# One kernel, one change: spreading the roots of the front's norms by a transpose, four masked copies and one product

## The chip, the cores and the metric

The kernel runs on one core of one Trainium2 chip. A core has five engines with instruction queues of their own: TensorE (PE in the profile; its weight loads are listed apart as PEld), VectorE (DVE), ScalarE (ACT), GpSimd (POOL) and SyncE (SP), which here only issues DMAs. The engines meet through semaphores. SBUF holds 128 partitions; PSUM has eight banks of 128 x 512 float32 into which TensorE writes.

The metric is the device time of one execution in microseconds. The kernel before was timed three times; its median is 1887.86 us.

## The reference, cut to what matters

One decoder block over 2048 tokens of width 1024. Every norm divides a token's row by the root of its mean square.

```python
def rmsnorm(x, g):
    r = lax.rsqrt(jnp.mean(xf * xf, axis=-1, keepdims=True) + EPS)
    return (xf * r * g).astype(x.dtype)

hn = rmsnorm(h, norm1_g)
proj = hn @ w_in                      # u_pool | q | k | v
y_pool = pool_mixer(u_pool, pool_w, pool_scale)
o = stick_breaking_attention(q, k, v)
mixed = concat([rmsnorm(y_pool, pool_out_g), rmsnorm(y_attn, attn_out_g)])
h = h + mixed @ w_out
hn2 = rmsnorm(h, norm2_g)
h = h + square(relu(hn2 @ w_up)) @ w_down
return rmsnorm(h, final_g)
```

## The kernel before, in words

All arithmetic is float32. The tokens stand along the free dimension, in four blocks of `T` = 512 (`NT` = 4); features lie on the 128 partitions. Each float32 operand of a product is split into a rounded part and the rest (`split`: a copy by ScalarE at L147, a subtraction by VectorE at L148), and a product is three matmuls on those parts (`products`, L179 to L181 in the front).

The program falls into the front, the up projection (L1135) and the down projection (L1308, L1485). The **front** holds the input projection, the pooling mixer, the attention (`near_unit`, L642 to L709) and the output projection with its residual. Its granules of work are listed in `prog` and emitted one after the other by `run`; between two of them, `catch_up` takes small pieces out of a list `later`, and `advance` takes pieces of attention. The Tile framework then orders each engine's instructions at build time, in a list schedule that runs on estimated durations; what stands in `tc.high_priority()` goes ahead of other work that is ready. On the chip each engine runs its instructions in that fixed order and waits where a semaphore makes it.

**A norm's root** takes these steps. Squares are summed over the features' chunks into a tile of 128 x 512 (`add_square`). `mean_squares` (L207) multiplies four 128 x 128 blocks of that sum by a column of 1/n: in PSUM there is then, for each of the four token blocks of 128, one column with one token to a partition. `inv_root` computes the inverse root in 128 x 4 elements, on GpSimd for all norms but the first (L223 to L226). The result is split into `yr`, 128 x 2 x 4: rounded part and rest, for each of four token blocks.

To be used, the root has to stand along the free dimension, on every partition. `to_all` does this: it takes a PSUM tile `pr`, calls `spread` (L233), and ScalarE copies `pr` to a tile `r` (L258). In `spread`, for each block and part, one column of `yr` is broadcast to 128 columns as the weights and multiplied with the identity: eight matmuls of 128 x 128, the two parts of a block adding up in its 128 columns of `pr`. VectorE then multiplies a chunk by its gain and by `r` (`normed`, L278; `put`, L862).

`to_all` is called fourteen times: for the first norm of block 0 directly from `inv_rms`, with VectorE as the engine of the root and the tag `px`; and thirteen times through `later_rms`, with a PSUM tile of the pools `pst` or `psz`: the first norm of blocks 1 to 3, the pooling norm and the attention norm of four blocks each, the second norm of blocks 0 and 1. The pools `pst` and `psz` have two banks each and are shared with the attention's transposes (L690) and logits (L642). After the spread, a gate makes the dense products that come twelve ticks later in `prog` stand behind it in TensorE's order.

The second norm of blocks 2 and 3 (L1143) and the last norm (L1360) call `spread` from the up and down projections. They are not part of `to_all`.

The pools of the front are opened in `open_pools`; `wp` is the last of its pools in SBUF on the right side. The constants stand in `const`; `ident` and `identr` are a 128 x 128 identity, and `gap` is an unused tile that keeps the places of what follows.

Of the kernel before, what the change touches and what calls it, by code (L numbers as in the profile page):

```python
# [8 lines left out]
F32 = mybir.dt.float32  # L9
F32R = mybir.dt.float32r  # L10
BF16 = mybir.dt.bfloat16
I32 = mybir.dt.int32
AF = mybir.ActivationFunctionType
ALU = mybir.AluOpType

P = 128
S = 2048
D = 1024
T = 512
# [8 lines left out]
TB = T // P  # L28
# [17 lines left out]
def hymba_block(ctx: ExitStack, tc: tile.TileContext, xT, gains, w_in, pool_w, w_out, w_up, w_down, out):  # L46
    nc = tc.nc
# [3 lines left out]
    const = pool("const", 1)  # L51
    vp = pool("vp", 2)
    dram = pool("dram", 1, space=bass.MemoryType.DRAM)
    wp = hpb = hpa = pa = bigp = x0p = ntp = tmp = att = psd = psx = psz = pst = pso = olp = accp = acc2p = acc3p = None

    def open_pools(scope):
        nonlocal hpb, wp, tmp, ntp, psd, psx, psz, pst, pso
        fpool = lambda name, bufs, **kw: scope.enter_context(tc.tile_pool(name=name, bufs=bufs, **kw))
        hpb = fpool("hpb", KD, side="right")
        ntp = fpool("ntp", 3, side="right")  # L60
        tmp = fpool("tmp", 2, side="right")
        wp = fpool("wp", 2, side="right")
        psz = fpool("psz", 2, space=PS)
        pso = fpool("pso", 1, space=PS)
        psd = fpool("psd", 2, space=PS)
        psx = fpool("psx", 1, space=PS)
        pst = fpool("pst", 2, space=PS)
# [19 lines left out]

    front_scope, left_scope, att_scope, out_scope, last_scope, inner = (ctx.enter_context(ExitStack()) for _ in range(6))
    open_pools(front_scope)
    open_big(left_scope)  # L90

# [3 lines left out]
    ident = const.tile([P, P], F32, name="ident")  # L95
    make_identity(nc, ident)
    identr = const.tile([P, P], F32R, name="identr")
    nc.vector.tensor_copy(identr, ident)
    const.tile([P, P // 2], F32, name="gap")
    later_keys = const.tile([P, 2, 2, P], mybir.dt.int8, name="later_keys")  # L100
    nc.gpsimd.memset(later_keys, 0.0)
    for i in range(2):
# [51 lines left out]
    marks, gates = {}, []  # L154
# [47 lines left out]
    def mean_squares(parts, n, where=None, tag="px"):  # L202

        pm = (where or psx).tile([P, T], F32, tag=tag, name="pm")
        for c in range(TB):
            for i, ss in enumerate(parts):
                marks["pm"] = nc.tensor.matmul(pm[:, c:c + 1], ss[:, c * P:(c + 1) * P], inv[n],  # L207
                                               start=(i == 0), stop=(i == len(parts) - 1))
        return pm[:, 0:TB]

    def inv_root(pm, eng):

        v, w = vp.tile([P, 3 * TB], F32, tag="v", name="v"), pm.shape[-1]
        m, y, t = v[:, 0:w], v[:, TB:TB + w], v[:, 2 * TB:2 * TB + w]
        nc.vector.tensor_scalar(m, pm, 1.0, EPS, op0=ALU.mult, op1=ALU.add)
        eng.tensor_scalar(y.bitcast(I32), m.bitcast(I32), -0.5, float(0x5F3759DF), op0=ALU.mult, op1=ALU.add)
        for _ in range(3):
            if eng is nc.vector:
                eng.scalar_tensor_tensor(t, y, -0.5, y, op0=ALU.mult, op1=ALU.mult)
                eng.tensor_tensor(t, t, m, ALU.mult)  # L220
                eng.scalar_tensor_tensor(y, t, 1.5, y, op0=ALU.add, op1=ALU.mult)
            else:
                eng.tensor_tensor(t, y, y, ALU.mult)  # L223
                eng.tensor_tensor(t, t, m, ALU.mult)
                eng.tensor_scalar(t, t, -0.5, 1.5, op0=ALU.mult, op1=ALU.add)
                eng.tensor_tensor(y, y, t, ALU.mult)  # L226
        return y

    def spread(pr, yr):

        for b in range(TB):
            for x in range(2):
                mm = nc.tensor.matmul(pr[:, b * P:(b + 1) * P], yr[:, x, b:b + 1].to_broadcast([P, P]), identr,  # L233
                                      start=(b == 0 and x == 0), stop=(b == TB - 1 and x == 1), skip_group_check=True)
        return mm

    def inv_rms(ss, n, r=None, eng=None, early=False):

        eng = eng or nc.gpsimd
        with tc.high_priority():  # L240
            y = inv_root(mean_squares([ss], n, psz if early else None, "pz" if early else "px"), eng)
            yr = tmp.tile([P, 2, TB], F32R, tag="yr", name="yr")
            eng.tensor_copy(yr[:, 0], y)
            eng.tensor_tensor(yr[:, 1], y, yr[:, 0].bitcast(F32), ALU.subtract)
            if eng is nc.vector:
                return to_all(yr, r, psx, "px")
            gates.append((state["tick"] + 10, marks["pm"]))
            return yr

    def to_all(yr, r, where, tag):  # L250
        with tc.high_priority():
            pr = where.tile([P, T], F32, tag=tag, name="pr")
            marks["pr"] = spread(pr, yr)
            if tag != "px":
                gates.append((state["tick"] + 12, marks["pr"]))
            if r is None:
                r = tmp.tile([P, T], F32, tag="r", name="r", bufs=2)
            nc.scalar.activation(r, pr, AF.Copy)  # L258
            return r

    def later_rms(at, key, ss, n, r=lambda: None, early=False):

        got = {}
        where = (psz, "pz") if early else (pst, "pt")
        later.append(lambda: got.update(yr=inv_rms(ss(), n, early=early)))
        later.append(None)
        later.append(lambda: at.update({key: to_all(got["yr"], r(), *where)}))

    def rms(chunks):
        return inv_rms(sum_squares(chunks), len(chunks) * P)  # L270
# [42 lines left out]
    todo, begun, finished, state = [], {}, set(), {"gran": 0, "tick": 0, "due": 0.0}  # L313
# [37 lines left out]
    def norm1_first():  # L351

        x, h = st[0]["x"], []
        for k in range(KD):
            d = make_h(0)
            a = nc.scalar.activation(d[:, 0], x[:, k], AF.Copy, scale=g1[:, k:k + 1])
            v = nc.vector.scalar_tensor_tensor(d[:, 1], x[:, k], g1[:, k:k + 1], d[:, 0].bitcast(F32),
                                               op0=ALU.mult, op1=ALU.subtract)
            h.append((d[:, 0], d[:, 1]))
        st[0]["h"] = h  # L360
        with tc.issue_after(a.ins), tc.issue_after(v.ins):
            ss = sum_squares([x[:, k] for k in range(KD)])
        st[0]["r"] = inv_rms(ss, D, root_tile(), nc.vector)
# [1247 lines left out]
    pa = inner.enter_context(tc.tile_pool(name="pa", bufs=2))  # L1611
    x0p = x0_scope.enter_context(tc.tile_pool(name="x0p", bufs=2, side="right"))
# [10 lines left out]
    with tc.If(got < count):  # L1623
        wlist.clear(), raws.clear(), grans.clear(), gates.clear(), marks.clear()
        state["gran"], last_split[0], last_mm[0], done[:] = 0, None, None, (None, None)
        open_pools(front_scope)
        open_big(left_scope)
        open_att(att_scope)
        for j in range(NT):
            far(j)  # L1630
        att_scope.close()
        open_last(front_scope, last_scope)
        open_out(out_scope)
        tail(False)
        run()
        ffn()
# [45 lines left out]
```

## Time and profile before

| | us |
|---|---|
| median of three runs | 1887.86 |
| the three runs | 1887.64 to 1891.71 |
| the profiled execution | 1888.39 |
| its span | 1886.4 |
| mean granted clock of TensorE | 0.997 |

The profile is that of one execution. Its span runs from the first to the last instruction; the time of an execution holds about 2 us more. A matmul's duration overlaps with its neighbours', so what it costs TensorE is read from the distance between starts on the timeline. In the rows of the views, a line such as L179 is a line of the kernel; then come the engine, the operation, the tiles written and read, the shape and the count. Behind a bar stand the busy time and the mean duration in ns, behind another bar the idle time of the engine before it and what ended it. In the rows of waits stand the waiter, what it waited for, the sum, the count and the longest, in us. On the timeline stand the start, the duration, and in brackets the engine's idle time before with what ended it.

### The profile page before, as it was taken

The numbers are of one execution on the slowest core, as the hardware profiler recorded it, in microseconds if no ns is written. First come the engines' busy times: TensorE is split into PE (matmuls) and PEld (weight loads), VectorE is DVE, ScalarE is ACT, GpSimd is POOL, SyncE is SP. The second block draws the span as 40 slices with busy tenths as digits, with TensorE's granted clock in tenths as the row PEclk, the third lists the DMA queues.
The fourth block names the chain that finished last, engine by engine and source line by source line (L and its number), as shares of the span: only waits on it lengthen the run. The fifth ranks groups of instructions, "written<-read, shape, count | busy, mean of one in ns | idle before, by whom it ended". The sixth has DMA issues, their size and how long they took to land.

```text
span 1886.4 us, 26655 instructions
## 1 busy us (share of the span) xinstructions
PE 1862.2 (99%) x8883; PEld 1550.0 (82%) x8883; DVE 1470.3 (78%) x2135; ACT 1024.9 (54%) x1616; POOL 227.8 (12%) x463
## 2 busy tenths in 40 slices
PE   9999999999999999999999999999999999999997
PEld 7888888888888888778888888887888888888886
DVE  6897889678866976777899988886666677888774
ACT  6565676466543554545566555554333665656543
POOL 0232234213311140000000000000010010020120
PEclk9999999999999999999999999999999999999998
DMA  6686796799796867888898988889999898999852
GB/s 225 221 269 186 236 294 206 254 338 304 273 370 226 319 202 272 312 282 286 309 357 299 341 293 284 290 298 335 372 325 333 269 320 306 331 304 344 283 202 92
DMA packets 222164, 535.91 MB, mean 284 GB/s; under 512 B 26048, under 2 KB 32192, under 8 KB 218176
## 3 DMA queue, kind: packets, MB, share of 16 engines
q1 hardware_dynamic: 217264, 525.46, 80.0%
q0 software_dynamic: 4608, 8.39, 2.5%
q8 instruction: 72, 1.18, 0.3%
q14 instruction: 76, 0.62, 0.1%
q10 hardware_dynamic: 144, 0.26, 0.0%
HBM read 349.46 MB, written 184.55 MB: 283 GB/s over the span
## 4 chain that ended last, share of the span: by engine, by line
PE 48%; DMA 6%; DVE 3%; issue 1%; ACT 1%; POOL 0%; SPq 0%; DVEq 0%; ACTq 0%
PE pb L1308 14%; PE pY L1135 12%; PE pb L1485 12%; PE pZ L1135 6%; PE pX L1135 3%; DMA ar<-sd 1%; DMA ar<-sdi 1%; DMA hn<-hs 1%; PE pb L1425 1%; DMA b<-in_w_down_dram 1%; DVE hw L148 0%; DMA td<-t 0%; DMA sdi<-a 0%; DMA t<-in_w_down_dram 0%; DMA rb<-in_w_up_dram 0%
## 5 line engine op out<-in xcount | busy, mean ns | idle before, releaser
L1135 PE MATMUL pY<-sa,hw 128*128 128x512 f32 x1536 | 366.5, 390 | 2.5 <-ACT u L1058 2.5
L1135 PEld LDWEIGHTS pY<-sa,hw 128*128 128x128 f32 x1536 | 287.8, 188 | 64.3 <-ACT u L1058 4.4
L1308 PE MATMUL pb<-ad,wd 128*128 128x512 f32 x1344 | 305.2, 389 | 0.4 <-DVE ad L148 0.4
L179 PE MATMUL pd<-h,hl 128*128 128x512 f32 x752 | 295.9, 394 | 1.2 <-DVE qk L148 1.1
L1308 PEld LDWEIGHTS pb<-ad,wd 128*128 128x128 f32 x1344 | 252.1, 188 | 53.4 <-DVE ad L148 1.1
L180 PE MATMUL pd<-h,hl 128*128 128x512 f32 x752 | 295.7, 393 | 0.0
L181 PE MATMUL pd<-h,hl 128*128 128x512 f32 x752 | 295.2, 393 | 0.0
L1485 PE MATMUL pb<-ad,wd 128*128 128x512 f32 x1104 | 253.9, 390 | 0.8 <-ACT ad L147 0.8
L1485 PEld LDWEIGHTS pb<-ad,wd 128*128 128x128 f32 x1104 | 206.5, 188 | 44.6 <-ACT ad L147 1.2
L148 DVE TENSOR_TENSOR ad<-ar,ad 128x1024 fp32r<-128x1024 f32 x160 | 194.0, 1220 | 42.8 <-ACT ad L147 42.4
L147 ACT ACTIVATE ad<-ar 128x1024 fp32r<-128x1024 f32 x160 | 168.9, 1057 | 92.6 <-PE pb L1485 31.9
L1135 PE MATMUL pZ<-sa,hw 128*128 128x512 f32 x768 | 186.9, 390 | 1.8 <-DVE a L1078 1.8
L1135 PEld LDWEIGHTS pZ<-sa,hw 128*128 128x128 f32 x768 | 143.8, 188 | 33.2 <-DVE a L1078 3.4
L147 ACT ACTIVATE hl<-raw 128x512 fp32r<-128x512 f32 x168 | 104.4, 629 | 116.7 <-PE pd L181 75.9
L179 PEld LDWEIGHTS pd<-h,hl 128*128 128x128 f32 x752 | 141.4, 188 | 28.5 <-DVE qk L148 1.5
L181 PEld LDWEIGHTS pd<-h,hl 128*128 128x128 f32 x752 | 141.3, 188 | 28.1
L180 PEld LDWEIGHTS pd<-h,hl 128*128 128x128 f32 x752 | 141.4, 188 | 25.9
L148 DVE TENSOR_TENSOR hl<-raw,hl 128x512 fp32r<-128x512 f32 x168 | 114.9, 689 | 50.5 <-ACT hl L147 49.2
L1052 ACT ACTIVATE a<-a 128x512 f32<-128x512 f32 x96 | 60.1, 629 | 95.2 <-DVE a L1094 42.2
L148 DVE TENSOR_TENSOR hw<-rt,hw 128x512 fp32r<-128x512 f32 x128 | 86.4, 684 | 24.4 <-ACT hw L147 24.3
L147 ACT ACTIVATE wd<-wq 128x1024 fp32r<-128x1024 f32 x56 | 59.5, 1063 | 77.4 <-PE pb L1308 67.0
L148 DVE TENSOR_TENSOR wd<-wq,wd 128x1024 fp32r<-128x1024 f32 x56 | 68.4, 1222 | 35.6 <-ACT wd L147 34.1
(224 smaller groups left out, 2709.7 us busy)
## 6 DMA issues: line engine op xcount, KB each, us to landing
ar<-sd SPq DMA_DIRECT2D x96, 512.0 KB, 5.7
ar<-sdi SPq DMA_DIRECT2D x64, 512.0 KB, 5.6
rb<-in_w_up_dram SPq DMA_DIRECT2D x30, 1024.0 KB, 6.6
sd<-a SPq DMA_DIRECT2D x104, 256.0 KB, 5.3
raw<-in_w_in_dram SPq DMA_DIRECT2D x50, 512.0 KB, 4.8
sdi<-hr SPq DMA_DIRECT2D x96, 256.0 KB, 5.4
wr<-in_w_down_dram SPq DMA_DIRECT2D x48, 512.0 KB, 5.6
sd<-s SPq DMA_DIRECT2D x88, 256.0 KB, 4.8
```

What stands on the lines that cost most here:

```text
L147: nc.scalar.activation(hi, src, AF.Copy)
L148: return nc.vector.tensor_tensor(lo, src, hi.bitcast(F32), ALU.subtract)
L179: nc.tensor.matmul(ps, hl[:, 0, c], hi, start=(k == 0), stop=False)
L180: nc.tensor.matmul(ps, hl[:, 0, c], lo, start=False, stop=False)
L181: last_mm[0] = nc.tensor.matmul(ps, hl[:, 1, c], hi, start=False, stop=(k == n - 1))
L1052: nc.scalar.activation(t, src, AF.Relu)
L1135: nc.tensor.matmul(t, w[:, wx, c], a[:, ax, c % 2], start=first and c == 0 and x == 0, stop=last and c == G - 1 and x == 2, skip_group_che ...
L1308: nc.tensor.matmul(b, t[:, wx, 2 * (kk % 2) + c, i * P:(i + 1) * P], a[:, ax, c], start=p in ("P1", "P5", "P2") and kk == 0 and c == 0 and ...
L1425: nc.tensor.matmul(b[:, cols], block(t, wx, c, n), a[:, ax, c, cols], start=False, stop=(i == 1 and c == 1 and x == 2), skip_group_check=True)
L1485: nc.tensor.matmul(ps[q, n], block(t, wx, c, n), left_[q][:, ax, c], start=(n_ in ("P1", "P3") and kk == 0 and c == 0 and x == 0), stop=(n ...
```

## The change

Thirteen of the fourteen calls of `to_all` (all but the one with the tag `px`) go through a new function, `spread_rows`. It transposes `yr`, seen as 128 x 8 columns (part by block), into eight rows of 128 in the first 128 columns of `pr`. ScalarE then copies these rows four times, into the four column blocks of a tile `roots` of 128 x 512, each time with a scale from a column of `sel` that is one for the two rows of that block and zero for the others. `roots` is zero elsewhere, so one product with weights of ones, over all 128 rows, adds the two parts of each token's root and puts the sum on every partition. It writes the whole of `pr`. ScalarE copies `pr` to `r` as before.

`roots` is one tile, cleared by GpSimd when the pools are opened. `sel` and the column of ones are two small constants, made by VectorE at the start; `gap` shrinks by their size.

```diff
+        roots = fpool("zp", 1, side="right").tile([P, T], F32R, name="roots")
+        nc.gpsimd.memset(roots.bitcast(F32), 0.0)
...
-    const.tile([P, P // 2], F32, name="gap")
+    const.tile([P, P // 2 - 8], F32, name="gap")
+    sel = const.tile([P, TB], F32, name="sel")
+    nc.vector.tensor_tensor(sel, ident[:, 0:TB], ident[:, TB:2 * TB], ALU.add)
+    oner = const.tile([P, TB], F32R, name="oner")
+    nc.vector.tensor_scalar(oner, sel, 0.0, 1.0, op0=ALU.mult, op1=ALU.add)
...
+    def spread_rows(pr, yr, r):
+
+        rows = 2 * TB
+        nc.tensor.transpose(pr[0:rows, 0:P], yr.bitcast(F32).rearrange("p x b -> p (x b)"), ident)
+        for b in range(TB):
+            nc.scalar.activation(roots[0:rows, b * P:(b + 1) * P], pr[0:rows, 0:P], AF.Copy, scale=sel[0:rows, b:b + 1])
+        mm = nc.tensor.matmul(pr, oner[:, 0:1].to_broadcast([P, P]), roots, start=True, stop=True)
+        nc.scalar.activation(r, pr, AF.Copy)
+        return mm
...
     def to_all(yr, r, where, tag):
         with tc.high_priority():
             pr = where.tile([P, T], F32, tag=tag, name="pr")
-            marks["pr"] = spread(pr, yr)
-            if tag != "px":
-                gates.append((state["tick"] + 12, marks["pr"]))
             if r is None:
                 r = tmp.tile([P, T], F32, tag="r", name="r", bufs=2)
-            nc.scalar.activation(r, pr, AF.Copy)
+            if tag == "px":
+                marks["pr"] = spread(pr, yr)
+                nc.scalar.activation(r, pr, AF.Copy)
+            else:
+                marks["pr"] = spread_rows(pr, yr, r)
+                gates.append((state["tick"] + 12, marks["pr"]))
             return r
```

More of the change, by code (lines that the diff above doesn't have):

```diff
@@ L53, in hymba_block @@
     dram = pool("dram", 1, space=bass.MemoryType.DRAM)
-    wp = hpb = hpa = pa = bigp = x0p = ntp = tmp = att = psd = psx = psz = pst = pso = olp = accp = acc2p = acc3p = None
+    wp = hpb = hpa = pa = bigp = x0p = ntp = tmp = att = psd = psx = psz = pst = pso = olp = accp = acc2p = acc3p = roots = None
     def open_pools(scope):
-        nonlocal hpb, wp, tmp, ntp, psd, psx, psz, pst, pso
+        nonlocal hpb, wp, roots, tmp, ntp, psd, psx, psz, pst, pso
         fpool = lambda name, bufs, **kw: scope.enter_context(tc.tile_pool(name=name, bufs=bufs, **kw))
```

## The prediction

> **What bounds the kernel now.** I read the page's first part, then the busy time of the two halves of the span, the waits of PE in the first of them, the answer for the line of the spreading product, and the timeline around single spreads. First the page: the span, then busy time, share and count of each engine.
>
> ```profile
> span 1886.4 us, 26655 instructions
> ...
> PE 1862.2 (99%) x8883; PEld 1550.0 (82%) x8883; DVE 1470.3 (78%) x2135; ACT 1024.9 (54%) x1616; POOL 227.8 (12%) x463
> ```
>
> The view of windows, split where the front ends (columns PE, PEld, DVE, ACT, POOL busy, then clock, DMA share, GB/s):
>
> ```profile
> 0.00:610.00 610.00, 604.05 (x3247) 509.68 (x3248) 482.38 (x776) 352.18 (x635) 153.42 (x356) 1.00 0.79 262
> ```
>
> TensorE runs without a break: 604.05 of the first 610 us, at the full clock. ScalarE has 610 − 352 = 258 us free there, VectorE 610 − 482 = 128 us. The waits of PE in the same 610 us, all of them:
>
> ```profile
> PE pzero L346 <- DVE zero L94: 1.5, 1, 1.5
> PE pd L494 <- ACT h L356: 1.1, 2, 0.6
> PE pd L179 <- DVE qk L148: 1.1, 2, 0.8
> PE po L702 <- DVE ot L660: 0.7, 1, 0.7
> PE pd L495 <- DVE h L357: 0.6, 2, 0.3
> PE pta L690 <- DVE at L148: 0.5, 1, 0.5
> PE pta L690 <- DVE sg L684: 0.4, 1, 0.4
> ```
>
> That is 5.9 us in ten waits, of which 3.2 us (L346, L494, L495) are the start. So in the front a microsecond less of work for PE is a microsecond less of time, as long as the order of its instructions leaves no new hole. Who waits in a spread (the answer for L233):
>
> ```profile
> L233 PE MATMUL pr<-identr,yr x136: 220/274/326, 36.2 to 1843.6; 128*128 128x128 f32 x136
> ...
> its engine sat idle before it (us, times) until:
>   POOL yr L1353: 2.2, 2
> who waited for it (us, times):
>   ACT r L258: 12.8, 9
>   ACT rf L1360: 4.0, 2
>   ACT ra L258: 1.8, 1
> ```
>
> 136 products are 17 spreads of 8: three of the last stage (L1360), which stay, and 14 through `to_all`. One of these has the tag `px` (the first block, 36 us) and keeps `spread`. **Thirteen change**, all before 607 us. PE waited for no front root (the two waits for `yr` are L1353's, at the end); ScalarE, in turn, stood waiting for the spread in ten cases, 14.6 us in all.
>
> **The change, part by part.** PE first. One spread of before on the timeline:
>
> ```profile
> 179.09 0.39 PE L180 MATMUL pd<-h,hl 128*128 128x512 f32 x1
> ...
> 179.31 0.39 PE L181 MATMUL pd<-h,hl 128*128 128x512 f32 x1
> ...
> 179.54 1.00 PE L233 MATMUL pr<-identr,yr 128*128 128x128 f32 x8
> ...
> 180.38 0.63 PE L690 MATMUL pta<-ident,sg 128*128 128x128 f32 x4
> ...
> 180.76 0.48 PE L179 MATMUL pd<-h,hl 128*128 128x512 f32 x1
> ```
>
> Durations overlap, so the cost on PE is the distance between starts. The eight small products hold PE from 179.54 to 180.38: **0.84 us**. A 128x512 product takes 179.31 to 179.54 = **0.23 us**. Four transposes against `ident`, of the kind that is added, take 180.38 to 180.76: 0.38/4 = **0.10 us** each. The new form is one such transpose and one 128x512 product: 0.10 + 0.23 = 0.33 us. Saved per spread 0.84 − 0.33 = 0.51 us; **13 × 0.51 = 6.6 us**.
>
> Bounds: the added transpose has only 8 columns of weights, which no row shows. The nearest narrower one has 64:
>
> ```profile
> 113.66 1.01 PE L233 MATMUL pr<-identr,yr 128*128 128x128 f32 x8
> ...
> 114.51 0.34 PE L702 MATMUL po<-at,vw 128*64 128x128 f32 x2
> ...
> 114.68 0.39 PE L181 MATMUL pd<-h,hl 128*128 128x512 f32 x1
> ...
> 114.70 0.60 ACT L258 ACTIVATE r<-pr 128x512 f32<-128x512 f32 x1 [2.94 <-PE pr L233]
> ```
>
> 0.17/2 = 0.085 us. (The same rows show a handoff: the spread ends at 114.67 and ScalarE, which had stood for 2.94 us, starts at 114.70.) At most the transpose costs its whole duration of 0.27 us (the 274 ns of L233's row) and the product its 0.39 us, with nothing overlapped: saving 0.84 − 0.66 = 0.18, 2.3 us in all. At least the transpose costs nothing: 0.61, 7.9 us. I take 0.10, the row of the same operation.
>
> The Trainium skill ("TensorE: Matmul & The Clock Gate", section "LDWEIGHTS (loading the stationary operand)") has the load of weights take its columns over 1.2 GHz, so 7 ns for 8 columns, and a 128-column stream about 56 ns. By these two figures the transpose would cost 0.06 us and the sum be 7.2 us; the trace's 64-column pair, at 0.085 us, costs more than its stream alone, so I stay with the row.
>
> ScalarE gets four more instructions per spread. Rows of the groups of ScalarE's instructions in the first 620 us (busy, mean ns | idle before):
>
> ```profile
> L147 ACT ACTIVATE at<-pta 128x512 fp32r<-128x512 f32 x56 | 33.3, 597 | 9.1 <-PE pta L690 7.7 <-PE po L702 1.0
> ...
> L425 ACT ACTIVATE yb<-pp,gains 128x512 f32<-128x512 f32 x16 | 11.0, 686 | 7.0 <-PE pp L424 6.9
> ...
> L258 ACT ACTIVATE r<-pr 128x512 f32<-128x512 f32 x12 | 7.2, 596 | 12.8 <-PE pr L233 12.8
> ...
> L463 ACT ACTIVATE vf<-pd 128x512 f32<-128x512 f32 x12 | 7.2, 596 | 17.3 <-PE pd L181 17.3
> ...
> L147 ACT ACTIVATE at<-pta 128x384 fp32r<-128x384 f32 x8 | 3.9, 493 | 1.7 <-PE pta L690 1.6
> ```
>
> From 512 to 384 columns 597 − 493 = 104 ns go, so 128 columns take 597 − 3 × 104 = 285 ns; a scale from a tile adds 686 − 596 = 90 ns (L425 against L258): an estimate of 0.375 us, four of them 1.5 us. Bounds: 1.1 us if the scale costs nothing at this size, 2.4 us if columns don't matter. 13 × 1.5 = 20 us more on ScalarE lie in its 258 free us. The closing copy (L258) stays.
>
> The path from `yr` to `r` grows: transpose 0.27, masks 1.5, two handoffs of 0.03, product 0.39, against 1.0 us for the eight: about 1.2 us later, plus what the product queues behind other work on PE. Who takes `r` are VectorE's multiplications (L278, L862); they come in program order, and none of PE's waits above is for what they make (`h`, `mix`), so I cost the later `r` at nothing and keep it as rival 2.
>
> At the start POOL clears a tile and VectorE makes two small constants. The timeline of the start:
>
> ```profile
> 0.94 0.53 POOL L101 MEMSET later_keys<- 128x512 int8 x1
> ...
> 5.45 0.69 DVE L148 TENSOR_TENSOR hl<-raw,hl 128x512 fp32r<-128x512 f32 x1 [3.20 <-ACT hl L147]
> ```
>
> A memset of 512 columns is 0.53 us; VectorE stands 3.2 us idle before 5.45, waiting for ScalarE and its load. I cost this at nothing; without that cover it would be about 0.7 us. The new 2 KB tile moves later tiles of the front by a multiple of 256 bytes, the smaller `gap` keeps the constants behind it in place: nothing.
>
> Sum: the profiled execution took 1888.39 us (span 1886.4 and 2.0 around it); 1888.39 − 6.6 = 1881.8, and I say **1882.0**, 0.3% under the median of 1887.86, which stands 0.5 us below the profiled execution.
>
> **The rivals.** (1) *The product makes PE wait.* PE takes its instructions in order; between transpose and product the order of the program, fixed at build time from estimated durations, must hold enough other matmuls. On the chip the masks need 0.27 + 1.5 + two handoffs, together 1.85 us, 8 products of 0.23 us. With k products between, PE stands 1.85 − 0.23k us per spread, and from k = 5 down (0.70 us) that is more than the 0.51 saved. With k = 0 it is 13 × (1.85 − 0.51) = +17.4 us: 1906; with k = 3 it is 13 × (1.16 − 0.51) = +8.5: 1897; with k = 5 or 6 it is 1888. Beside it stands the Trainium skill (same page, "Step-by-step: what each phase is for"): only weight loads are pulled ahead, matmuls stay in program order, so that all work behind the product would stand too.
> Against it speaks the nearest chain of PE, one ScalarE instruction and PE that the trace has, a copy `vf` and its transposes, at the shortest of its 12 times:
>
> ```profile
> 356.40 0.59 ACT L463 ACTIVATE vf<-pd 128x512 f32<-128x512 f32 x1
> ```
>
> ```profile
> 359.49 0.38 PE L466 MATMUL ptv<-ident,vf 128*128 128x128 f32 x2
> ```
>
> The copy ended at 356.99, its taker started 2.5 us later, so the planned order leaves more room than the chip needs: over 3 us for one instruction of 0.6. None of the ten waits above is for such a copy (L466), nor for a root. For it speaks that a root is put ahead of all other work as soon as it counts as ready, and that four short instructions may be estimated closer than one long one. If ScalarE comes late to the masks, PE waits too: in four of fourteen spreads it was not waiting for PE.
>
> (2) *The later `r` costs elsewhere.* VectorE and ScalarE wait in order for the roots; the rows above show 14.6 us of such waits on ScalarE. A second wait, for the product behind the masks, may double them, and holds the PSUM bank, shared with the transposes of attention, some 2 us longer. If a third of 13 × 1.5 = 20 us came through to PE, it would be 6.5 us: 1888, no change.
>
> (3) *The sum is right, but the planned order falls differently.* The ten waits above were worth 2.7 us after the start; other ones of that size move the time by 2 us to either side.
>
> (4) *The change doesn't do what it says*, if the work saved were not on the path. With 604 of 610 us busy I give this nothing.
>
> **How the numbers follow.** Forecast, 1880 to 1884: 0.58. Rivals 1 and 2 at break-even, 1884 to 1891.6: 0.27. Rival 1 with few products between, 1892 to 1906: 0.13. A larger gain, by the bound of 7.9 us and luck in the order, under 1880: 0.02. A measurement of this kernel can tell about 0.2%, 3.8 us: faster than 1884.1 is 0.60, within 0.27, slower than 1891.6 0.13. The range of 8 in 10 leaves out the slower case and the far low end, and runs from **1879.5 to 1890**.
>
> **What would show it.** Right: 13 transposes and 13 products of 128x512 in place of 104 small ones, none of them in the waits of PE; PE's busy time in the front some 6.6 us shorter and the first product of the next stage that much earlier. The masks at 0.3 to 0.4 us each. Wrong: a wait of PE for the masked tile (rival 1), or new waits of PE for split tiles or PSUM banks, with VectorE or ScalarE standing for `pr` or `r` (rival 2); or a transpose or product that costs more than 0.33 us together.

## The result, and the profile after

The change made the kernel slower. Over eight runs each, the median is 1901.24 us against 1889.11 us; the ratio is 1.0054 with an interval of 1.0041 to 1.0066, so about 10 us are lost (the medians alone lie 12.1 us apart) where 6.6 were to be gained. The profiled execution took 1901.87 us; its span is 1900.1 us, 13.7 more than before.

First the new operations themselves (the answer for the tiles `roots` and `pr` of the changed kernel; durations in ns are minimum, median and maximum):

```profile
L248 ACT ACTIVATE roots<-pr,sel x52: 341/343/361, 71.2 to 619.8; 8x128 fp32r<-8x128 f32 x52
...
L246 PEld LDWEIGHTS pr<-ident,yr x13: 83/84/85, 69.7 to 618.4; 128*8 128x8 f32 x13
L246 PE MATMUL pr<-ident,yr x13: 270/271/276, 69.9 to 618.6; 128*8 128x128 f32 x13
L249 PEld LDWEIGHTS pr<-roots,oner x13: 185/188/188, 72.3 to 624.2; 128*128 128x128 f32 x13
L249 PE MATMUL pr<-roots,oner x13: 389/389/503, 72.3 to 624.4; 128*128 128x512 f32 x13
```

Thirteen transposes, thirteen products and 52 masked copies of 0.343 us stand there. One spread, on the timeline of TensorE and then of ScalarE:

```profile
232.05 0.39 PE L185 MATMUL pd<-h,hl 128*128 128x512 f32 x1
232.28 0.27 PE L246 MATMUL pr<-ident,yr 128*8 128x128 f32 x1
232.31 0.48 PE L186 MATMUL pd<-h,hl 128*128 128x512 f32 x1
232.62 0.40 PE L187 MATMUL pd<-h,hl 128*128 128x512 f32 x1
...
237.17 0.39 PE L249 MATMUL pr<-roots,oner 128*128 128x512 f32 x1
237.40 0.40 PE L185 MATMUL pd<-h,hl 128*128 128x512 f32 x1
```

```profile
232.59 1.11 ACT L248 ACTIVATE roots<-pr,sel 8x128 fp32r<-8x128 f32 x4 [0.59 <-PE pr L246]
...
238.43 0.61 ACT L250 ACTIVATE r<-pr 128x512 f32<-128x512 f32 x1
```

From 232.05 to 232.62 lie the transpose and two products of 0.23 us, so the transpose costs 0.11 us; the spread's product costs 237.17 to 237.40 = 0.23 us. The masks are done at 233.70, but TensorE comes to the product only at 237.17, with 25 other matmuls in between. From the transpose to the end of the copy to `r` there are 239.04 − 232.28 = 6.8 us. Over the thirteen spreads the mean from the first matmul of a spread to the end of `r` is 6.7 us; before, it was 1.8 us.

The waits of TensorE between 16 and 665 us, all of them (before, this view has 1.1, 0.7, 0.5, 0.4 and 0.2 us, 2.9 in sum):

```profile
PE pd L185 <- DVE qk L154: 6.8, 2, 5.6
PE pd L185 <- DVE qkr L467: 1.5, 1, 1.5
PE pr L249 <- ACT roots L248: 1.5, 1, 1.5
PE pd L187 <- DVE hl L154: 0.9, 1, 0.9
PE pd L185 <- ACT hl L153: 0.7, 1, 0.7
PE pp L440 <- ACT pls L153: 0.4, 1, 0.4
PE pp L441 <- DVE pls L154: 0.4, 2, 0.3
PE pz L660 <- issue: 0.3, 1, 0.3
PE po L720 <- DVE ot L678: 0.2, 1, 0.2
```

12.7 us, and only 1.5 of them are the product waiting for the masked tile. The longest wait is at 249 us. Its chain, on the timelines of SyncE, ScalarE, VectorE and TensorE, a fence for each:

```profile
243.66 0.38 SPq L488 DMA_DIRECT2D vs<-vt  x1
```

```profile
249.22 0.63 ACT L153 ACTIVATE mix<-nt 128x512 fp32r<-128x512 f32 x1 [3.54 <-DMA vs<-vt]
...
252.86 0.60 ACT L153 ACTIVATE qk<-pd 128x512 fp32r<-128x512 f32 x1
```

```profile
253.97 0.67 DVE L154 TENSOR_TENSOR qk<-pd,qk 128x512 fp32r<-128x512 f32 x1
```

```profile
254.70 0.79 PE L185 MATMUL pd<-h,hl 128*128 128x512 f32 x1 [5.57 <-DVE qk L154]
255.29 0.63 PE L186 MATMUL pd<-h,hl 128*128 128x512 f32 x1
255.72 0.63 PE L187 MATMUL pd<-h,hl 128*128 128x512 f32 x1
```

A normed chunk (`mix`) takes one of three `st` buffers, in turn with `qk`, `vt` and `pls`. Its buffer was last used by a `vt` tile, whose DMA was issued at 243.66. ScalarE stands in front of this copy for 3.54 us, and seven instructions behind it is the copy that frees a PSUM bank of the dense product (`qk`, 252.86). TensorE waits for that bank for 5.57 us. Before, the same copy of `mix` waited 1.53 us for the same DMA, at 241.75, and TensorE 0.85.

The late root has a part in this. VectorE's order, before and after:

```profile
229.62 2.07 DVE L278 SCALAR_TENSOR_TENSOR nt<-yb,gains,r 128x512 f32<-128x512 f32 x3
...
236.13 0.67 DVE L148 TENSOR_TENSOR vt<-ptv,vt 128x512 fp32r<-128x512 f32 x1
```

```profile
239.47 2.15 DVE L296 SCALAR_TENSOR_TENSOR nt<-yb,gains,r 128x512 f32<-128x512 f32 x3
...
242.15 0.68 DVE L154 TENSOR_TENSOR vt<-ptv,vt 128x512 fp32r<-128x512 f32 x1
```

Three multiplications by `r`, which ended at 239.04, now stand just ahead of the subtraction that completes `vt`; before, it came 4.4 us behind them. From ScalarE's part of `vt` to the issue of its first DMA 4.3 us pass now, before 1.7; and the second DMA took 5.5 us to land where it had taken 4.5.

The rows after the wait show a second price: products start 0.43 us apart, where 0.23 is usual. The windows of the changed kernel, cut where the granted clock changes (the column before the DMA share is the clock):

```profile
0.00:8.20 8.20, 5.32 (x13) 1.87 (x13) 3.21 (x28) 3.25 (x4) 2.41 (x12) 1.00 0.66 195
8.20:15.00 6.80, 6.51 (x15) 4.59 (x15) 5.96 (x11) 6.34 (x11) 0.00 (x0) 0.50 1.03 375
15.00:254.00 239.00, 230.76 (x1211) 194.42 (x1209) 191.94 (x320) 144.74 (x272) 53.16 (x117) 1.00 0.71 227
254.00:260.80 6.80, 6.10 (x17) 4.84 (x17) 4.92 (x9) 2.94 (x6) 0.40 (x2) 0.50 0.81 247
260.80:704.60 443.80, 435.57 (x2283) 366.20 (x2282) 349.39 (x515) 255.05 (x467) 113.73 (x257) 1.00 0.82 279
704.60:708.00 3.40, 3.40 (x11) 2.82 (x11) 1.23 (x1) 0.00 (x0) 0.00 (x0) 0.50 0.00 0
```

Three stretches at half clock, of 6.8, 6.8 and 3.4 us; before had none in its span but one after the end of its matmuls. The second and third follow long waits. The third belongs to the up projection, where TensorE waits for the root of the last block:

```profile
698.20 1.00 PE L239 MATMUL pr<-identr,yrlast 128*128 128x128 f32 x8
699.04 0.67 PE L1153 MATMUL pX<-sa,hw 128*128 128x512 f32 x2
704.06 1.21 PE L239 MATMUL pr<-identr,yrlast 128*128 128x128 f32 x5 [4.34 <-POOL yrlast L869]
```

That spread isn't part of the change. Before, it ran at 706.09 us, 9.0 us behind its root; in the new plan five of its eight products were pulled ahead, to a place that TensorE reached 4.3 us before their root was there.

**The balance.** The up projection began at 674.06 us before and at 683.68 us after: +9.6 us. In that stretch TensorE's waits (with the start) went from 6.1 to 15.9 us, +9.8; the two half-clock stretches cost half of the time in which TensorE worked in them, (6.51 + 6.10)/2 = 6.3 us. So the work itself shrank by 9.8 + 6.3 − 9.6 = **6.5 us**, the 6.6 of the prediction. Behind it the span is 4.1 us longer: 4.3 us of the wait for `yrlast` and 1.7 of half clock, less the 1.9 that remain for all other places. The half-clock stretch at 8.2 us, 3.3 us of the 13.7, has no wait of the change ahead of it and shows in some profiles of other kernels too (st4, upfix); it would account for the profiled pair differing by more than the ratio.

### The profile page after: what moved, and what is told of

It is laid out like the page before. It is cut to its first block, busy times and chain, and to the rows that moved or that the text cites. A ratio compares the mean times of both kernels' runs of the same rounds, so it can differ in the third digit from the quotient of the medians.

```text
span 1900.1 us, 26522 instructions
## 1 busy us (share of the span) xinstructions
PE 1862.6 (98%) x8805; PEld 1547.3 (81%) x8805; DVE 1470.7 (77%) x2137; ACT 1038.7 (55%) x1668; POOL 217.7 (11%) x464
## 4 chain that ended last, share of the span: by engine, by line
PE 43%; DVE 3%; DMA 2%; issue 1%; ACT 1%; POOL 0%; SPq 0%; DVEq 0%; ACTq 0%
PE pb L1326 16%; PE pb L1503 12%; PE pY L1153 8%; PE pZ L1153 4%; PE pX L1153 2%; DMA td<-t 1%; PE pb L1443 1%; DVE hw L154 0%; DMA ar<-sd 0%; DMA wr<-in_w_down_dram 0%; DMA sdi<-hr 0%; DMA sdi<-a 0%; DMA hr<-sd 0%; DVE t L1054 0%; DVE sa L154 0%
```

## The experiments

Three theories. **Latency**: the roots come later, norm chunks meet buffers and queues at a worse time, and TensorE waits behind them. **Replanning**: the build-time order of the whole front and of the up projection changed, and any new order has bad places. **Placement**: the new tile and the constants shift addresses. All runs were made beside runs of the kernel before on the same chip; ratios are to those.

| run | ratio to before (95%) | TensorE's waits, 16 to 665 us | mean from root to `r` |
|---|---|---|---|
| before | 1 | 2.9 | 4.6 |
| the change | 1.0054 (1.0041 to 1.0066) | 12.7 | 10.0 |
| place | 0.9996 (0.9982 to 1.0009) | 4.8 | 4.6 |
| chain | 1.0052 (1.0033 to 1.0070) | 7.2 | 10.3 |
| st4 | 1.0041 (1.0026 to 1.0056) | 7.7 | 10.1 |
| upfix0 | 1.0000 (0.9989 to 1.0010) | 5.1 | 4.7 |
| upfix | 1.0017 (1.0005 to 1.0030) | 12.2 | 10.0 |
| hrows_u | 1.0005 (0.9995 to 1.0015) | 4.6 | 7.9 |
| mrows_u | 1.0010 (1.0000 to 1.0020) | 8.6 | 6.8 |
| nudge_u | 0.9999 (0.9988 to 1.0010) | 2.2 | 4.8 |
| q1 | 0.9997 (0.9986 to 1.0008) | 11.1 | 9.5 |
| q2v | 0.9967 (0.9956 to 0.9978) | 6.2 | 6.7 |
| q2p | 1.0013 (1.0002 to 1.0025) | 9.9 | 5.0 |

The waits are the sums of each profile's view; the last column, in us, is the mean over thirteen spreads from the end of the last GpSimd instruction on `yr` to the end of the copy to `r`, the roots and the copies paired in their order. Before, place and upfix0 have the same order of TensorE's instructions in the front, and 2.9, 4.8 and 5.1 us of waits: profiles of one order differ by that much.

**place.** Only tile, memset and constants are left of the change.

```diff
-                marks["pr"] = spread_rows(pr, yr, r)
+                marks["pr"] = spread(pr, yr)
+                nc.scalar.activation(r, pr, AF.Copy)
```

> Only the new tile, its memset, the two constants and the smaller gap stay; all fourteen spreads are the eight small products again. TensorE's, ScalarE's and SyncE's planned order is that of before. If the 2 KB shift or the constants cost the time (theory of placement): most of the 10 us stay, 1897 to 1901. If the later roots (latency) or the new order of the plan (replanning) cost it: 1888, ratio 1.000 within 0.0015, and the same few waits of TensorE as before.

Measured 1888.74 us, 0.9996. Placement is out: the 2 KB shift, the memset and the constants together cost nothing that this interval (0.9982 to 1.0009) would show.

**short.** One product with a column of the root as weights; no transpose, no masks.

```diff
-        nc.tensor.transpose(pr[0:rows, 0:P], ...)
-        for b in range(TB):
-            nc.scalar.activation(roots[0:rows, ...], pr[0:rows, 0:P], AF.Copy, scale=...)
-        mm = nc.tensor.matmul(pr, oner[:, 0:1].to_broadcast([P, P]), roots, start=True, stop=True)
+        mm = nc.tensor.matmul(pr, yr[:, 0, 0:1].to_broadcast([P, P]), roots, start=True, stop=True)
```

> The transpose and the four masks are left out; one 128x512 product with the root's first column as weights writes pr, so r holds no root of the tokens and the output isn't the reference's. TensorE does 13 x 0.61 = 7.9 us less than before and r comes no later than before. Latency theory: 1881, ratio 0.996, TensorE's waits in the front as before (about 3 us after the start). Replanning theory: the gain is eaten in part by new waits at other places, 1882 to 1895, with waits of TensorE of some us that have nothing to do with a late root.

The whole time, 3945 us, says nothing: without true roots the program also enters its last branch, which fetches far keys and does the tail again. The first pass can be read. Its up projection begins 6.2 us earlier than before (674.06):

```profile
667.90 0.84 PE L1149 MATMUL pY<-sa,hw 128*128 128x512 f32 x3
```

with 4.8 us of waits in the front, two more than before. So work saved on TensorE does come through in the front when the roots are on time (4.5 us behind, in the mean of this run). But at 685 us this kernel, too, waits 3.9 us for `yrlast`: that wait needs no late root.

**chain.** The late chain without the saving.

```diff
-        mm = nc.tensor.matmul(pr, oner[:, 0:1].to_broadcast([P, P]), roots, start=True, stop=True)
+        for b in range(TB):
+            for x in range(2):
+                mm = nc.tensor.matmul(pr[:, b * P:(b + 1) * P], (oner, zeror)[x][:, 0:1].to_broadcast([P, P]),
+                                      roots[:, b * P:(b + 1) * P], ...)
```

> Transpose, four masks and late r as in the change, but the one product is cut into eight of 128x128 again (four of them with weights of zeros): TensorE does 13 x 0.1 = 1.3 us more than before, and nothing is saved. Latency theory: the waits of the changed kernel come back (about 249 us, behind mix and a DMA of vt) and the time is that of the changed kernel plus 7.9: 1905 to 1910. Replanning theory: the waits fall elsewhere, and the time is anywhere from 1890 to 1910.

Measured 1900.24 us, ratio 1.0052: with 0.61 us more work in each of thirteen spreads it is as slow as the change, not slower by 7.9 us. Its wait near 250 us was 1.1 us, not 5.6, so the waits did not come back unchanged. The changed kernel has 7.9 us less work than this one behind the same late chain, and gained nothing by it: its profile has 5.5 us more of waits in the front, and 17 us at half clock (6.8 of them at the start) where this one has 6.8. The spread of the last root waits 4.3 us in both.

**st4.** Four `st` buffers.

```diff
-        d = pa.tile([P, 2, T], F32R, tag="st", ..., bufs=3)
+        d = pa.tile([P, 2, T], F32R, tag="st", ..., bufs=4)
...
-    sslast = const.tile([P, T], F32, name="sslast")
+    sslast = rlast[:, 1]
```

> The changed kernel with four st buffers in place of three (the sum of squares of the last block shares its place with a root tile that is written later, to make room). Latency theory with the st buffers as its place: ScalarE's wait of mix for the DMA of vt (3.5 us at 249) and TensorE's wait of 5.6 us behind it go, with the 3.1 us of half clock after it: 1892 to 1894, ratio to before 1.002. Replanning theory: the waits move, time within 4 us of the changed kernel, 1897 to 1903.

1896.56 us, 1.0041; the interval overlaps that of the change. By the theory ScalarE's wait of `mix` for the DMA of `vt` should have gone. It did not,

```profile
248.30 0.63 ACT L153 ACTIVATE mix<-nt 128x512 fp32r<-128x512 f32 x1 [4.37 <-DMA vs<-vt]
```

but TensorE's wait behind it fell to 3.4 us, and the one at 427 us is no longer there. One more buffer moves the collision by a chunk. Still, the front got shorter: the up projection begins at 675.44 us, 8.2 us earlier than in the changed kernel (1.7 of them from a shorter half-clock stretch at the start) and 1.4 later than before. What was gained there is hidden by the up projection, where the wait for `yrlast` is 5.3 us here, with 6.8 us at half clock. Buffers of their own for `mix` were not tried.

**upfix and upfix0.** In the up projection, the spread of a last root is held behind the matmuls of its group; in the changed kernel and in the kernel before.

```diff
-                    nc.tensor.matmul(t, w[:, wx, c], ...)
+                    group = nc.tensor.matmul(t, w[:, wx, c], ...)
...
-                spread(pr, yrlast[:, i])
+                with tc.issue_after(group.ins):
+                    spread(pr, yrlast[:, i])
```

> The changed kernel; in the up projection the spread of each last root is held behind the matmuls of its own group (group 6 and group 10), so that the second can't be planned ahead of its root. The front's order is untouched. Replanning theory: TensorE's wait of 4.3 us for yrlast goes, with the half clock behind it (1.7 us): 6 us less than the changed kernel, about 1895, ratio to before 1.002. If that wait only moves to another place of the up projection: 1901, ratio 1.005.

> The kernel before with the same hold in the up projection, the control. Before had no wait there, so both theories: 1889, ratio 1.000 within 0.002. If the hold by itself gains or costs something, it shows here and is taken off the run above.

1894.51 us, 1.0017, against 1.0000 for the control. The hold takes 6.7 us (1901.24 − 1894.51; by the two ratios 7.0) off the changed kernel, where 6 were expected, and the wait for `yrlast` is gone. So about two thirds of the loss sat in a spread that the change doesn't touch. The front of this run has the order of the changed kernel and the same late chain, and 12.2 us of waits.

**hrows_u and mrows_u.** With the hold; the new form in one half of the calls.

```diff
+    def later_rms(at, key, ss, n, r=lambda: None, early=False, rows=True):
...
+            if tag == "px" or not rows:
+                marks["pr"] = spread(pr, yr)
```

> With the hold; the transpose, masks and product only in the seven calls whose root goes to h, to the residual or to the last attention norms (first norm of blocks 1 to 3, second norm of 0 and 1, attention norm of 2 and 3). The six norms of the front that go through the st buffers (pooling 0 to 3, attention 0 and 1) keep the eight products. Saved on TensorE: 7 x 0.51 = 3.6 us. If late roots hurt where mix waits for st buffers: that wait (249) is back to under 1 us, 1885.5, ratio 0.998. If the front's losses come of any new plan: 1889 or more, with waits of some us at other places.

> With the hold; the opposite half: the new form in the six norms that go through the st buffers, the eight products in the other seven. Saved 6 x 0.51 = 3.1 us. If late roots hurt at the st buffers: TensorE's wait near 245 to 250 is 4 to 6 us plus up to 3 us of half clock, 1891 to 1894, ratio 1.002. If not: 1886, ratio 0.998.

1.0005 and 1.0010. In the first the wait near 245 us is 1.7 us and that at 139 us is gone, in the second they are 2.4 (with half clock behind it) and 1.7 us: the late roots of the norms that go through the `st` buffers bring back these two, as the latency theory has it, though smaller, and at 245 us by 0.7 us alone. But the first did not gain its 3.6 us: it has the product's wait for the masks at 68 us (1.2), and behind 665 us, in a plan that is new there too, 0.8 us more of waits than before and two stretches at half clock (3.4 us near 693, 6.8 us near 1320; about 4.9 us lost by them).

**nudge_u.** With the hold; an unused transpose ahead of the eight products.

```diff
-        for b in range(TB):
-            nc.scalar.activation(roots[0:rows, ...], pr[0:rows, 0:P], AF.Copy, scale=...)
-        mm = nc.tensor.matmul(pr, oner[:, 0:1].to_broadcast([P, P]), roots, start=True, stop=True)
+        mm = spread(pr, yr)
```

> With the hold; the eight products stay and each of the thirteen spreads gets one unused transpose in front, no masks, no second handoff: TensorE does 13 x 0.1 = 1.4 us more than before. Latency theory: 1890 to 1891, ratio 1.0007, front waits as before. Replanning theory: a new plan by itself costs some us: 1893 or more.

0.9999, with 2.2 us of waits. A slightly different plan costs nothing by itself. It is hardly a new one, though: counted from the traces (TensorE's instructions ahead of the up projection by the tiles they name, a spread as one), some 30 of 3440 are out of the order of before. In hrows_u, mrows_u, short and q2p it is some 200, in q2v 330, in the change, chain and st4 380 to 400. So this run does not show that a plan as new as the change's would cost nothing.

**q1.** With the hold; one multiplication by VectorE in place of four copies.

```diff
-        for b in range(TB):
-            nc.scalar.activation(roots[0:rows, b * P:(b + 1) * P], pr[0:rows, 0:P], AF.Copy, scale=sel[0:rows, b:b + 1])
+        nc.vector.tensor_tensor(roots[0:rows] as (b n), pr[0:rows, 0:P] repeated over b, sel[0:rows] repeated over n, ALU.mult)
```

> With the hold; the four masked copies of ScalarE are one multiplication by VectorE (8 x 512, about 0.7 us in place of 1.1). The same two handoffs, in and out of TensorE. If the length of the masks makes the roots late: r comes earlier and the waits of TensorE at 139, 249 and 424 fall to half, 1890, ratio 1.000. If it is the second handoff to TensorE, which the plan puts some 25 matmuls behind whatever lies between: product still 4 to 5 us behind the transpose, time as the changed kernel with the hold, 1893 to 1896, ratio 1.002.

0.9997, 1890.50 us. The expectation of the first theory gave this time, but not its reason: the waits did not halve (11.1 us in place of 12.2), and the root came only 0.5 us earlier. What differs from upfix in the profiles is the clock: q1 has no half-clock stretch before the end of its matmuls, upfix has five; over all executions the mean granted clock has a median of 0.997 in q1 and 0.995 in upfix. So waits of this sum, at full clock, are nearly paid for by the work saved: 8.2 us more than before against 6.5.

**q2v and q2p.** With the hold; no transpose: the identity, repeated for four blocks, is multiplied by the root's columns by VectorE (q2v) or GpSimd (q2p), rounded part and rest, and two 128x512 products with weights of ones write `pr`.

```diff
+        eye = ident repeated over 4 blocks
+        for x in range(2):
+            nc.vector.tensor_tensor((roots, roots2)[x], eye, yr[:, x] repeated over 128 columns, ALU.mult)   # q2p: nc.gpsimd
+        for x in range(2):
+            mm = nc.tensor.matmul(pr, ones_w, (roots, roots2)[x], start=(x == 0), stop=(x == 1))
```

> With the hold; no transpose and no second handoff to TensorE: VectorE multiplies an identity, repeated for four blocks, by the root's columns (rounded part, then the rest), and two 128x512 products with weights of ones write pr. TensorE does 13 x (0.84 - 0.46) = 4.9 us less than before, r comes later than before by two VectorE instructions alone. Latency theory: front waits of TensorE as before (3 to 5 us), 1884 to 1885, ratio 0.9975. Replanning theory: its front has some 560 changed rows of TensorE's order, so waits come up again, 1888 to 1893, ratio 1.000 to 1.002.

> As the run above, with the two multiplications on GpSimd, which is free but slower (about 1 to 1.5 us each, an estimate from its 0.8 us for 128 x 256). r is 2 to 3 us later than before, half as late as in the changed kernel. Latency theory: between the two, 1886 to 1889, ratio 0.999. Replanning theory: its order differs less from before (360 rows), so it is no worse than the run above.

q2v is the version that beats both: 1884.07 us, 0.9967 (0.9956 to 0.9978). One row of the view of `roots` shows its price on VectorE:

```profile
L250 DVE TENSOR_TENSOR roots<-ident,yr x26: 679/692/862, 66.1 to 603.1; 128x512 fp32r<-128x512 f32 x26
```

26 × 0.69 = 18 us of VectorE, hidden in its idle time, against 4.9 us less on TensorE; the gain, 0.33% or 6.2 us, is a little more than this. It is not all explained: in the profiles, 2.5 of the 6.5 us by which the span is shorter lie ahead of the up projection (671.60 against 674.06 us) and 4.0 behind it, where this form changes nothing. q2p lost, 1.0013, although its `r` comes hardly later than before: here the latency theory fails. Its 26 instructions on GpSimd take 1.04 us, and VectorE's waits for the attention mask of GpSimd rose from 7.8 to 12.1 us; that these caused its loss is argued, not shown.

## Why the prediction was wrong, point by point

**What bounds the kernel: right, but read too far.** TensorE is the bound, and work taken off it comes through, as short and q2v show. It doesn't follow that nothing else can become the bound: before had only 2.9 us of waits in the order that it had, which does not say that the other engines had room at each place.

**The cost of the parts: right.** Transpose 0.11 (0.10 forecast), product 0.23 (0.23), four masks 1.11 us (1.5, within the bounds 1.1 to 2.4), and 6.5 us of work saved (6.6). The Trainium skill ("TensorE: Matmul & The Clock Gate", section "LDWEIGHTS (loading the stationary operand)") has the load take its columns over 1.2 GHz, 7 ns for 8. The trace does not agree: this load shows 84 ns, and the transpose stands for 0.11 us, where the estimate by the page was 0.06. Loads of 64 and 128 columns (L720, L249) show 135 and 187 ns in the mean, so a column costs here nearly what the page says, and some 80 ns come on top.

**The step that failed** is the one on the path from `yr` to `r`: "about 1.2 us later, plus what the product queues behind other work on PE", which was costed "at nothing". The root came 5.4 us later in the mean (10.0 against 4.6), since in twelve of the thirteen spreads the product stands 25 to 34 other matmuls, 5 to 6.6 us, behind the transpose in the planned order. And the front was not free of new waits, as that term needed: with the start they rose by 9.8 us, though how much of it the later root makes is open (below). The evidence lay in the prediction itself: the copy `vf`, whose taker started 2.5 us after it, was used to show that the product would not make TensorE wait (it did in one spread of thirteen, 1.5 us), and the same row says that whoever needs the product gets it that much later. Room on the engine that is ahead is lateness for the one behind.

**Rival 2 came nearest**: a later `r` that costs elsewhere. Its place is seen at 249 us: ScalarE in order, a chunk of the late norm in front, a bank of the dense product behind it; only that the chunk waits there for a buffer, not for its root. Rival 2 was put at 6.5 us, to end near 1888; the front's waits rose by 9.8. That a long wait can also lower the clock for 3.4 or 6.8 us was not in the sum at all.

What the experiments settle for the front: not placement (place), not the number or the engine of the masks (q1 has nearly the same lateness and nearly the same waits). Kernels with all thirteen roots 9.5 to 10.3 us behind had 7 to 13 us of waits in the front, those with roots on time 2 to 5, with q2p as the exception. But the kernels with the late roots are also those whose order changed most, and no run has late roots without a changed order. q2v comes nearest to the reverse: much of the order changed, roots 2.1 us later, 6.2 us of waits. At 249 us the trace shows how a late root takes part; how much of the front's waits is lateness and how much is another order at some few places near 139, 249 and 425 us stays open, and so does why q2p has them.

**Rival 3 was mis-sized**: a plan that falls differently was put at 2 us to either side. The second spread of the last roots alone cost 4.3 us of wait and 1.7 us of half clock, and holding it in its place took 6.7 us off the time.

**Rival 1** gave a time near the measured one, 1897 to 1906, for a reason that cost 1.5 us in one spread and nothing in twelve.

## What to carry to other kernels

Where an order is made at build time, a detour from the bound engine through another and back costs little of its work and much of its latency: ask who takes the result, and what stands behind that taker in its queue, before costing the lateness at nothing. Where a saving is smaller than one wait of the kind that the plan can make, look after the change for new waits in stages that it doesn't touch, and hold those instructions in their place before judging it. A form that keeps the producer's side off the bound engine (q2v: the diagonal is built by VectorE from SBUF) gained more from a smaller saving, though part of that gain lies where the form changes nothing.

## What the runs showed of the hardware that had not been expected

A wait of TensorE costs more than itself. Behind the start, stretches at half of the granted clock followed waits of 1.6 to 5.6 us, and lasted 3.4 or 6.8 us. The shortest such wait is that of chain. Its row on TensorE's timeline, and the windows of 3.41 us before and behind the point where its clock fell:

```profile
70.39 0.33 PE L253 MATMUL pr<-roots,oner 128*128 128x128 f32 x1 [1.59 <-ACT roots L250]
```

```profile
68.93:72.34 3.41, 1.95 (x13) 1.78 (x14) 3.04 (x7) 2.58 (x7) 0.20 (x1) 1.00 0.34 135
72.34:75.75 3.41, 3.41 (x10) 2.63 (x9) 3.41 (x7) 2.52 (x4) 0.59 (x1) 0.50 0.01 2
```

When a wait does this can be worked out from the traces. In each profile the stretches begin on one grid: in the changed kernel at 8.25, 254.01 and 704.57 us, which lie 72 and 132 times 3.413 us apart. In chain's window ahead of its stretch TensorE was idle for 3.41 − 1.95 = 1.46 us. In the thirteen profiles other than short, and behind their first 4 us, every window of the grid with more than 1.8 us of idle time was followed by half clock (thirteen of them), none with less than 1.3 us was, and in between both occur. So a wait counts by what of it falls into one window. The 2.08 us of upfix that end at 141.77 fell into one window, and the clock went down; the 2.35 us of q1 that end at 250.62 were split by the grid at 249.02 into 0.75 and 1.60 us, and it stayed full.

The Trainium skill ("TensorE: Matmul & The Clock Gate", section "Part 1: The HAM clock gate (the "warmup" mystery)") tells of a free-running window of about 3.4 us after which an idle TensorE falls back to half clock. The lengths of the stretches, 3.4 and 6.8 us, and their grid agree; that a window idle for only about half of its time was enough here is what the runs add.
